# Gate and up projection of a feature tile as seven block products instead of eight, with the order of every engine written out

## The chip, the cores and the metric

The kernel runs on one core of a Trainium2 chip. The time is device microseconds (us) of one execution. Five engines work from queues of their own, each in order: TensorE (PE, its weight loads PEld), VectorE (DVE), ScalarE (ACT), GpSimd (POOL) and SyncE (SP, which only issues transfers here).

## What is computed

Two layers of an encoder on 768 tokens (512 of one batch, 256 of another). Each layer has four mixers, which the change doesn't touch, and then a gated feed-forward block of width 2816 on a model width of 1024:

```python
for l in range(DEPTH):
    ...
    x = x + _rms(mix, p['norm_mix_post'][l])
    h = _rms(x, p['norm_ffn_pre'][l])
    f = (jax.nn.silu(h @ p['ffn_w_gate'][l]) * (h @ p['ffn_w_up'][l])) @ p['ffn_w_down'][l]
    x = x + _rms(f, p['norm_ffn_post'][l])
```

## The kernel before

Each fp32 operand is held as a high part, rounded to the format that PE multiplies (`whi`, `hh`, `ah`), and a low part, the rest (`wlo`, `hl`, `al`). A product is three matmuls: high by high, high by low, low by high. `hh` and `hl` hold the normalised activations, features on the partitions: 8 chunks of 128 by 768 tokens.

The 2816 features are 22 tiles of 128. For each tile `ffn_up` computes gate (`fg`) and up (`fu`), each as 8 chunks by 3 matmuls, for 512 and for 256 tokens: 96 matmuls, 48 of 512 columns and 48 of 256. ACT takes the tanh, DVE makes the product `th`, ACT and DVE split it into `ah` and `al`. Two tiles make a group. `ffn_down` multiplies the group's activations by its down weights, 6 token tiles by 2 halves, 6 matmuls of 512 columns each (`dn`), and DVE adds each result to `y`. So per tile there are 6 such sets of six.

Weights come in pieces of 128x1024 (512 KB), three per tile, into two buffers `raw` by loads on the SP queue. `piece` splits one: ACT copies the high part, then DVE or POOL, in turn, subtracts to get the low part. A `raw` buffer can be loaded again when that subtraction is done.

A scheduler that works by estimates of durations sets the order of every engine. The first group goes through the tokens as 512 and then 256, the last as 256 and then 512, so that the closing norms of the 256 (`post_norm`, `pre_norm`) lie beside the products of the 512. In the middle groups the matmuls of one tile run between the `dn` matmuls of the group before.

Of the kernel before, what the change touches and what calls it, by code (L numbers as in the profile page):

```python
# [82 lines left out]
class Trunk:  # L83
    def __init__(self, ctx, tc, xp, xs, wp, pv, bc, par, cst, scan, strips, yp, ys):
# [1109 lines left out]
    def ffn_up(self, l, f, seqs, wg, wu, th, ah, al):  # L1194
        nc = self.nc
        part = len(seqs) < 2
        pg, pu = {}, {}

        def gate(s):
            t0, n, *_r = SEQS[s]  # L1200
            c = slice(t0, t0 + n)
            nc.scalar.activation(th[:, c], pg[s][:, :n], AF.Tanh, scale=0.5)  # L1202
            nc.vector.scalar_tensor_tensor(out=th[:, c], in0=th[:, c], scalar=1.0, in1=pg[s][:, :n], op0=ALU.add, op1=ALU.mult)

        for s in seqs:
            pg[s] = self.bank("pS" if part else "pb", f"fg{l}_{f}_{s}")
            if not part:
                self.feat_mm(pg[s][:, :SEQS[s][1]], *wg, P, *SEQS[s][:2])
                gate(s)
        for s in seqs:  # L1210
            t0, n, *_r = SEQS[s]
            c = slice(t0, t0 + n)
            pu[s] = self.bank("pS", f"fu{l}_{f}_{s}")
            if part:

                for a in range(0, n, 256):
                    self.feat_mm(pg[s][:, a:a + 256], *wg, P, t0 + a, 256)
                    self.feat_mm(pu[s][:, a:a + 256], *wu, P, t0 + a, 256)
                gate(s)
            else:  # L1220
                self.feat_mm(pu[s][:, :n], *wu, P, t0, n)
            nc.vector.scalar_tensor_tensor(out=th[:, c], in0=th[:, c], scalar=0.5, in1=pu[s][:, :n], op0=ALU.mult, op1=ALU.mult)  # L1222
        c = slice(SEQS[seqs[0]][0], SEQS[seqs[-1]][0] + SEQS[seqs[-1]][1])
# [237 lines left out]
```

## Time and profile before

| | |
|---|---|
| median of the runs | 2311.38 us |
| lowest run | 2308.88 us |
| the profiled execution, its own time | 2307.11 us |
| its span, first to last instruction | 2305.3 us |
| PE busy | 2195.2 us (95%) |
| DVE, ACT, POOL busy | 1278.9, 803.9, 577.7 us |
| mean granted clock of PE | 0.981 |

The span holds, twice, some 580 us of mixers and some 570 us of feed-forward. Busy times of PE are from the start of a matmul to its modelled end; matmuls overlap, so the rate is read from one start to the next. On the other engines a row's duration is the time for which the engine is taken.

### The profile page before, as it was taken

The numbers are of one execution on the slowest core, as the hardware profiler recorded it, in microseconds if no ns is written. First come the engines' busy times: TensorE is split into PE (matmuls) and PEld (weight loads), VectorE is DVE, ScalarE is ACT, GpSimd is POOL, SyncE is SP. The second block draws the span as 40 slices with busy tenths as digits, with TensorE's granted clock in tenths as the row PEclk, the third lists the DMA queues.
The fourth block names the chain that finished last, engine by engine and source line by source line (L and its number), as shares of the span: only waits on it lengthen the run. The fifth ranks groups of instructions, "written<-read, shape, count | busy, mean of one in ns | idle before, by whom it ended". The sixth has DMA issues, their size and how long they took to land.

```text
span 2305.3 us, 44071 instructions
## 1 busy us (share of the span) xinstructions
PE 2195.2 (95%) x18072; PEld 1940.4 (84%) x18072; DVE 1278.9 (55%) x2404; ACT 803.9 (35%) x1675; POOL 577.7 (25%) x521
## 2 busy tenths in 40 slices
PE   7999989999999999999999999898999999999997
PEld 7888888878888888888888888787888888888886
DVE  5597658785623333333566875688764333433345
ACT  4333335665421112221243433455663211221211
POOL 1342213334311111111233422123352111111113
PEclk9999999999999999999999999999999999999999
DMA  4543564345422111222225535634263211122112
...
DMA packets 245096, 240.95 MB, mean 105 GB/s; under 512 B 138784, under 2 KB 191904, under 8 KB 244896
## 3 DMA queue, kind: packets, MB, share of 16 engines
...
q8 instruction: 142, 2.33, 0.4%
...
## 4 chain that ended last, share of the span: by engine, by line
PE 37%; DVE 7%; DMA 3%; issue 1%; POOL 1%; ACT 1%; SPq 0%; DVEq 0%; POOLq 0%; ACTq 0%
PE fg L194 8%; PE fu L194 8%; PE dn L1236 8%; PE dz L194 3%; PE op L183 2%; PE za L183 1%; PE zb L183 1%; DVE nper L460 1%; DVE el L458 1%; PE sd L171 1%; DMA bd<-sl 1%; PE zv L183 1%; PE ob L171 0%; DMA fb<-yd 0%; PE pg L171 0%
## 5 line engine op out<-in xcount | busy, mean ns | idle before, releaser
L165 POOL TENSOR_TENSOR wlo<-raw,whi 128x1024 fp32r<-128x1024 f32 (+1 forms) x108 | 258.5, 2393 | 1049.7 <-ACT whi L162 858.5
L1242 DVE TENSOR_TENSOR y<-y,dn 128x512 f32<-128x512 f32 x240 | 162.7, 686 | 341.7 <-PE dn L1236 341.0
L162 ACT ACTIVATE whi<-raw 128x1024 fp32r<-128x1024 f32 (+1 forms) x222 | 225.3, 1021 | 334.2 <-DMA raw<-in_wp_dram 127.0
L194 PE MATMUL fg<-hl,whi 128*128 128x256 f32 (+1 forms) x768 | 250.3, 326 | 1.4 <-DVE hl L208 1.4
L194 PE MATMUL fg<-hh,whi 128*128 128x256 f32 (+1 forms) x768 | 250.0, 325 | 0.7 <-ACT hh L207 0.7
L194 PE MATMUL fg<-hh,wlo 128*128 128x256 f32 (+1 forms) x768 | 249.0, 325 | 0.0
L194 PE MATMUL fu<-hl,whi 128*128 128x256 f32 (+1 forms) x768 | 248.3, 323 | 0.0
L194 PE MATMUL fu<-hh,whi 128*128 128x256 f32 (+1 forms) x768 | 248.2, 323 | 0.0
L194 PE MATMUL fu<-hh,wlo 128*128 128x256 f32 (+1 forms) x768 | 247.9, 323 | 0.0
L165 DVE TENSOR_TENSOR wlo<-raw,whi 128x1024 fp32r<-128x1024 f32 (+1 forms) x114 | 154.8, 1357 | 132.6 <-ACT whi L162 130.1
L1236 PE MATMUL dn<-whi,ah 128*128 128x512 f32 x528 | 208.9, 396 | 1.9 <-DVE y L1242 1.9
L1236 PE MATMUL dn<-wlo,ah 128*128 128x512 f32 x528 | 209.3, 396 | 0.0
L1236 PE MATMUL dn<-whi,al 128*128 128x512 f32 x528 | 203.8, 393 | 0.0
L194 PEld LDWEIGHTS fg<-hl,whi 128*128 128x128 f32 x768 | 146.1, 190 | 16.0 <-DVE hl L208 1.8
L194 PEld LDWEIGHTS fg<-hh,whi 128*128 128x128 f32 x768 | 146.0, 190 | 15.7 <-ACT hh L207 0.9
L194 PEld LDWEIGHTS fg<-hh,wlo 128*128 128x128 f32 x768 | 146.1, 190 | 13.4
L194 PEld LDWEIGHTS fu<-hh,wlo 128*128 128x128 f32 x768 | 145.4, 189 | 13.7
L194 PEld LDWEIGHTS fu<-hl,whi 128*128 128x128 f32 x768 | 145.6, 190 | 13.6
L194 PEld LDWEIGHTS fu<-hh,whi 128*128 128x128 f32 x768 | 145.6, 190 | 13.1
L1224 ACT ACTIVATE ah<-th 128x768 fp32r<-128x768 f32 (+2 forms) x52 | 38.6, 742 | 298.3 <-DVE th L1222 298.3
L1202 ACT ACTIVATE th<-fg 128x512 f32<-128x512 f32 (+1 forms) x88 | 42.7, 485 | 235.9 <-PE fg L194 235.4
L1236 PEld LDWEIGHTS dn<-whi,al 128*128 128x128 f32 x528 | 98.7, 188 | 23.4
...
## 6 DMA issues: line engine op xcount, KB each, us to landing
...
```

The source lines that it names most:

```text
L162: nc.scalar.activation(hi[:, :n], raw[:, :n], AF.Copy)
L165: eng.tensor_tensor(out=lo[:, :n], in0=raw[:, :n], in1=hi[:, :n].bitcast(F32), op=ALU.subtract)
L171: self.nc.tensor.matmul(ps[c], lhsT=lhsT[:, c], rhs=rhs, start=start, stop=stop)
L183: mm(ps, lhsT=a, rhs=b[:, c:c + ncol], start=i == 0, stop=i == tot - 1)
L194: mm(ps, lhsT=a, rhs=b, start=i == 0, stop=i == 3 * NK - 1)
L458: V.tensor_tensor(out=ev, in0=q[:, j + 1:32, j:j + 1].to_broadcast([96, m, j]), in1=q[:, j:j + 1, 0:j].to_broadcast([96, m, j]), op=ALU.mult)
L460: V.tensor_tensor(out=q[:, j + 1:32, 0:j], in0=q[:, j + 1:32, 0:j], in1=ev, op=ALU.add)
L1202: nc.scalar.activation(th[:, c], pg[s][:, :n], AF.Tanh, scale=0.5)
L1224: nc.scalar.activation(ah[:, c], th[:, c], AF.Copy)
L1236: nc.tensor.matmul(ps, lhsT=a[p], rhs=w[q], start=i == 0, stop=i == tot - 1)
L1242: nc.vector.tensor_tensor(out=yt, in0=yt, in1=ps, op=ALU.add)
```

## The change

Write the gate and up weights of a tile as a block matrix: row blocks gate and up, column blocks chunks 0 to 3 and 4 to 7 of the model width, A11 and A12 for gate, A21 and A22 for up. Write the activations as blocks too: chunks 0 to 3 and 4 to 7 by tokens 0 to 383 and 384 to 767, B11, B12, B21, B22. The four results are then made from seven block products (Winograd's form of Strassen's scheme) in place of eight. Weight sums are S1 = A21 + A22, S2 = S1 - A11, S3 = A11 - A21, S4 = A12 - S2. Activation sums are T1 = B12 - B11, T2 = B22 - T1, T3 = B22 - B12, T4 = T2 - B21. The products are 1: A11 B11, 2: A12 B21, 3: S4 B22, 4: A22 T4, 5: S1 T1, 6: S2 T2, 7: S3 T3. A block product (`block_mm`) is 4 chunks by 3 matmuls of 384 columns.

Tiles 0 and 1 of a layer stay as they were, and tiles 2 to 21 take the new form. In `ffn_sums` the activation sums are formed and split once per layer: POOL and DVE form them and DVE and ACT split them, and T1 is written over B12 in `hh` and `hl` once tiles 0 and 1 have read it. `ffn_units` writes out the order of all engines for tiles 2 to 21. The two raw pieces of a tile, x = (A11, A21) and y = (A22, A12), are split and summed in place: `first` splits A11 (names whr, wlr), `second` splits y (wha, wla), `sums` makes S1 to S4 on POOL in x and y, `third` splits the new x (whb, wlb), `fourth` the new y (whc, wlc). `down_split` splits a half of the down weights (whd, wld), and the two `raw` buffers serve x, y and the down half in turn. The seven products go into six PSUM banks in turn, and DVE and ACT combine them in `fg` and `fu`. The `dn` sets stand one by one between the products. Tiles 2 and 3 have no `dn` sets beside them, as the first group's are done before. The last group's `dn` sets and all closing norms come after tile 21.

```diff
-FFG = 2
+HT = TOK // 2
...
+TS_TAGS = ("Q", "T", "T", "T", "Z", "Z", "V", "D", "D", "Q", "Q")
+XF_ORDER = (0, 1, 2, 4, 5, 3)
...
+    def ffn_sums(self, l):
+        nc = self.nc
+        V, S, A = nc.vector, nc.scalar, nc.gpsimd
+        F = lambda x: x.bitcast(F32)
+        L, R = slice(0, HT), slice(HT, TOK)
+        units = [self.slot(tag, [P, 2, HT], f"ts{l}_{i}", F32R) for i, tag in enumerate(TS_TAGS)]
+        cells = [u[:, j] for u in units for j in range(2)]
+        cells += [self.slot("z", [P, HT], f"tz{l}_{i}", F32R) for i in range(2)]
+        t1s = [self.tmp(f"t1{l}_{j}").rearrange("p (k c) -> p k c", k=2) for j in range(2)]
+        self.tt = {}
+        for k in range(4):
+            t1 = t1s[k // 2][:, k % 2]
+            t2, t3, t4 = [self.slot("R", [P, 512], f"t{n}{l}_{k}")[:, :HT] for n in (2, 3, 4)]
+            for eng, o, r, c in ((A, t1, k, L), (A, t3, k, R), (V, t2, 4 + k, R), (V, t4, 4 + k, L)):
+                eng.tensor_tensor(out=o, in0=F(self.hh[:, r, c]), in1=F(self.hl[:, r, c]), op=ALU.add)
+            A.tensor_tensor(out=t1, in0=t3, in1=t1, op=ALU.subtract)
+            A.tensor_tensor(out=t3, in0=t2, in1=t3, op=ALU.subtract)
+            V.tensor_tensor(out=t2, in0=t2, in1=t1, op=ALU.subtract)
+            V.tensor_tensor(out=t4, in0=t2, in1=t4, op=ALU.subtract)
+            for n, x in ((2, t2), (3, t3), (4, t4)):
+                hi, lo = cells.pop(0), cells.pop(0)
+                S.activation(hi, x, AF.Copy)
+                V.tensor_tensor(out=lo, in0=x, in1=F(hi), op=ALU.subtract)
+                self.tt[n, k] = hi, lo
+        for k in range(4):
+            t1, hi = t1s[k // 2][:, k % 2], self.hh[:, k, R]
+            S.activation(hi, t1, AF.Copy)
+            V.tensor_tensor(out=self.hl[:, k, R], in0=t1, in1=F(hi), op=ALU.subtract)
+    def block_h(self, n, k):
+        if n in (2, 3, 4):
+            return self.tt[n, k]
+        row, c = {1: (k, slice(HT, TOK)), "11": (k, slice(0, HT)), "21": (4 + k, slice(0, HT)), "22": (4 + k, slice(HT, TOK))}[n]
+        return self.hh[:, row, c], self.hl[:, row, c]
...
+    def ff_split(self, eng, tags, name, x):
+        hi, lo = [self.slot(t, [P, x.shape[1]], f"{n}{name}", F32R) for n, t in zip(("wh", "wl"), tags)]
+        self.nc.scalar.activation(hi, x, AF.Copy)
+        eng.tensor_tensor(out=lo, in0=x, in1=hi.bitcast(F32), op=ALU.subtract)
+        return hi, lo
+    def block_mm(self, name, w, j, n):
+        ps = self.bank(("pb", "pb", "pS", "pS", "pT", "pO")[self.nbank % 6], name)[:, :HT]
+        self.nbank += 1
+        i = 0
+        for k in range(4):
+            wh, wl = [x[:, j * 512 + k * P:j * 512 + (k + 1) * P] for x in w]
+            bh, bl = self.block_h(n, k)
+            for a, b in ((wh, bh), (wh, bl), (wl, bh)):
+                self.nc.tensor.matmul(ps, lhsT=a, rhs=b, start=i == 0, stop=i == 11)
+                i += 1
+        return ps
...
+    def down_mm(self, l, g, t, n, act, w):
+        ps = self.bank("pa", f"dn{l}_{g}_{t}_{n}")
+        i = 0
+        for j, (ah, al) in enumerate(act):
+            a = ah[:, t * P:(t + 1) * P], al[:, t * P:(t + 1) * P]
+            b = [x[:, j * 512:(j + 1) * 512] for x in w]
+            for p, q in ((0, 0), (0, 1), (1, 0)):
+                self.nc.tensor.matmul(ps, lhsT=a[p], rhs=b[q], start=i == 0, stop=i == 5)
+                i += 1
+        return ps, g, t, n
...
+    def ffn_units(self, l):
+        nc = self.nc
+        V, S, A = nc.vector, nc.scalar, nc.gpsimd
+        LO, HI = slice(0, 512), slice(512, 1024)
+        L, R = slice(0, HT), slice(HT, TOK)
+        raw, w = {}, {}
+        add = lambda o, x, y, op=ALU.add: V.tensor_tensor(out=o, in0=x, in1=y, op=op)
+        def load(f, i):
+            raw[f, i] = self.ff_raw(l, f // 2, 2 * (f % 2) + i, "raw")
+        def first(f):
+            w[f, "r"] = self.ff_split(V, ("R", "R"), f"r{l}_{f}", raw[f, 0][:, LO])
+        def second(f):
+            w[f, "a"] = self.ff_split(A, ("whi", "wlo"), f"a{l}_{f}", raw[f, 1])
+        def sums(f):
+            x, y = raw[f, 0], raw[f, 1]
+            A.tensor_tensor(out=y[:, LO], in0=x[:, HI], in1=y[:, LO], op=ALU.add)
+            A.tensor_tensor(out=x[:, HI], in0=x[:, LO], in1=x[:, HI], op=ALU.subtract)
+            A.tensor_tensor(out=x[:, LO], in0=y[:, LO], in1=x[:, LO], op=ALU.subtract)
+            A.tensor_tensor(out=y[:, HI], in0=y[:, HI], in1=x[:, LO], op=ALU.subtract)
+        def third(f):
+            w[f, "b"] = self.ff_split(V, ("whi", "wlo"), f"b{l}_{f}", raw.pop((f, 0)))
+        def fourth(f):
+            w[f, "c"] = self.ff_split(V, ("whi", "wlo"), f"c{l}_{f}", raw.pop((f, 1)))
+        def down_load(g, n):
+            raw["d"] = self.ff_raw(l, g, 4 + n, "raw")
+        def down_split(g, n, tags=("X", "X")):
+            w["d", g, n] = self.ff_split(A, tags, f"d{l}_{g}_{n}", raw.pop("d"))
+        load(2, 0)
+        load(2, 1)
+        first(2)
+        second(2)
+        sums(2)
+        third(2)
+        acts, tail, due = {}, None, []
+        def settle(keep=0):
+            while len(due) > keep:
+                self.down_add(*due.pop(0))
+        for f in range(2, NF):
+            nxt = f + 1 if f + 1 < NF else None
+            g, odd = f // 2, f % 2
+            G, U = self.tmp(f"fg{l}_{f}"), self.tmp(f"fu{l}_{f}")
+            c11, c12, c21, c22 = G[:, L], G[:, R], U[:, L], U[:, R]
+            downs = [] if g == 1 else [(t, odd) for t in range(NT)]
+            def mm(n, key, j, h):
+                return self.block_mm(f"p{n}{l}_{f}", w[f, key], j, h)
+            def down(n=1):
+                for _i in range(n):
+                    if downs:
+                        t, half = downs.pop(0)
+                        due.append(self.down_mm(l, g - 1, t, half, acts[g - 1], w["d", g - 1, half]))
+            def tanh(x):
+                th = self.slot("R", [P, 512], f"ft{l}_{f}")[:, :HT]
+                S.activation(th, x, AF.Tanh, scale=0.5)
+                return th
+            def gate(th, x):
+                V.scalar_tensor_tensor(out=x, in0=th, scalar=1.0, in1=x, op0=ALU.add, op1=ALU.mult)
+            def up(x, u):
+                V.scalar_tensor_tensor(out=x, in0=x, scalar=0.5, in1=u, op0=ALU.mult, op1=ALU.mult)
+            wd = (g - 1, 1) if not odd and g > 1 else (g, 0) if odd else None
+            if tail:
+                tail()
+            settle()
+            fourth(f)
+            p = mm(1, "r", 0, "11")
+            S.activation(c12, p, AF.Copy)
+            if nxt:
+                load(nxt, 1)
+            if wd:
+                if "d" not in raw:
+                    down_load(*wd)
+                down_split(*wd)
+            if nxt:
+                load(nxt, 0)
             else:
+                down_load(g, 1)
+            p = mm(2, "a", 1, "21")
+            if odd:
+                down()
+            add(c11, c12, p)
+            th = tanh(c11)
+            p = mm(4, "a", 0, 4)
+            down()
+            settle(1)
+            gate(th, c11)
+            S.activation(c21, p, AF.Copy)
+            p = mm(6, "b", 0, 2)
+            down()
+            settle(1)
+            if nxt:
+                second(nxt)
+            else:
+                down_split(g, 1, ("whi", "wlo"))
+            add(c12, c12, p)
+            p = mm(7, "b", 1, 3)
+            down()
+            settle(1)
+            if nxt:
+                first(nxt)
+                sums(nxt)
+            add(c22, c12, p)
+            add(c21, c22, c21, ALU.subtract)
+            up(c11, c21)
+            p = mm(5, "c", 0, 1)
+            down()
+            settle(1)
+            add(c12, c12, p)
+            add(c22, c22, p)
+            p = mm(3, "c", 1, "22")
+            down(2)
+            if nxt:
+                third(nxt)
+            nwd = (g, 0) if not odd else (g, 1)
+            if nxt:
+                down_load(*nwd)
+            settle(1)
+            add(c12, c12, p)
+            th = tanh(c12)
+            def tail(f=f, g=g, c11=c11, c12=c12, c22=c22, G=G, th=th, gate=gate, up=up):
+                gate(th, c12)
+                up(c12, c22)
+                hi, lo = [self.slot("D", [P, TOK], f"{n}{l}_{f}", F32R) for n in ("ah", "al")]
+                S.activation(hi, G, AF.Copy)
+                V.tensor_tensor(out=lo, in0=G, in1=hi.bitcast(F32), op=ALU.subtract)
+                acts.setdefault(g, []).append((hi, lo))
+        tail()
+        settle()
+        return acts[NF // 2 - 1], [w["d", NF // 2 - 1, n] for n in range(2)]
...
+        self.ffn_sums(l)
+        act = [t[1:] for t in tiles]
+        wd = [self.piece(l, PIECE_FF + 4 + n, tags=("X", "X")) for n in range(2)]
+        for t in range(NT):
+            for n in range(2):
+                self.down_add(*self.down_mm(l, 0, t, n, act, wd[n]))
+        with self.tc.manual_schedule():
+            act, wd = self.ffn_units(l)
+        g_post, g_next = (*self.gains(l, 3), None) if last else self.gains(l, 3, 4)
+        for t in XF_ORDER:
+            for n in range(2):
+                self.down_add(*self.down_mm(l, NF // 2 - 1, t, n, act, wd[n]))
+            x = self.slot(XF_TAG[t], [P, DM], f"xf{l}_{t}")
+            nc.sync.dma_start(out=x, in_=self.x1[t])
...
+    wg, wu = [f[name].reshape(L, NK, P, NF, P).transpose(0, 3, 2, 1, 4) for name in ("ffn_w_gate", "ffn_w_up")]
+    dn = f["ffn_w_down"].reshape(L, NF, P, 2, 512)
+    for i in range(NF):
+        at = PIECE_FF + 6 * (i // 2) + 2 * (i % 2)
+        x, y = wg[:, i], wu[:, i]
+        if i >= 2:
+            x, y = np.concatenate([x[:, :, :4], y[:, :, :4]], axis=2), np.concatenate([y[:, :, 4:], x[:, :, 4:]], axis=2)
+        wp[:, at], wp[:, at + 1] = x.reshape(L, P, -1), y.reshape(L, P, -1)
+    for g in range(NF // 2):
+        for n in range(2):
+            wp[:, PIECE_FF + 6 * g + 4 + n] = np.concatenate([dn[:, 2 * g, :, n], dn[:, 2 * g + 1, :, n]], axis=2)```

DVE in the middle of layer 0. First before, around the end of tile 10; `y` are the sums of the down projection, `wlo` low parts of weights:

```order
L1242 TENSOR_TENSOR y_3_6776<-y_3_6776,dn_8_3_1_9732 128x512
L1222 SCALAR_TENSOR_TENSOR th_10_9772<-th_10_9772,fu_10_1_9870 128x256
L1225 TENSOR_TENSOR al_10_9774<-th_10_9772,ah_10_9773 128x768
L1242 TENSOR_TENSOR y_4_6777<-y_4_6777,dn_8_4_0_9740 128x512
L1242 TENSOR_TENSOR y_4_6777<-y_4_6777,dn_8_4_1_9748 128x512
L1242 TENSOR_TENSOR y_5_6778<-y_5_6778,dn_8_5_0_9756 128x512
L1203 SCALAR_TENSOR_TENSOR th_11_9775<-th_11_9775,fg_11_0_9910 128x512
L1242 TENSOR_TENSOR y_5_6778<-y_5_6778,dn_8_5_1_9764 128x512
L165 TENSOR_TENSOR wlo_70_10021<-raw_70_10018,whi_70_10020 128x1024
```

And DVE after, the second half of tile 11 (`p` are products, `ft` the tanh):

```order
L1245 TENSOR_TENSOR wlr_12_10219<-raw_6_0_10123,whr_12_10218 128x512
L1304 TENSOR_TENSOR fu_11_10091<-fg_11_10090,p_11_10197 128x384
L1304 TENSOR_TENSOR fu_11_10091<-fu_11_10091 128x384
L1371 SCALAR_TENSOR_TENSOR fg_11_10090<-fg_11_10090,fu_11_10091 128x384
L1293 TENSOR_TENSOR y_3_6776<-y_3_6776,dn_4_3_1_10210 128x512
L1304 TENSOR_TENSOR fg_11_10090<-fg_11_10090,p_11_10229 128x384
L1304 TENSOR_TENSOR fu_11_10091<-fu_11_10091,p_11_10229 128x384
L1245 TENSOR_TENSOR wlb_12_10273<-raw_6_0_10123,whb_12_10272 128x1024
L1293 TENSOR_TENSOR y_4_6777<-y_4_6777,dn_4_4_1_10242 128x512
L1304 TENSOR_TENSOR fg_11_10090<-fg_11_10090,p_11_10252 128x384
```

DVE has the low parts of tile 12's weights between the steps of tile 11, and the steps of tile 11 stand behind them.

POOL in the same place. Before, it has only low parts of weights, every second piece:

```order
L165 TENSOR_TENSOR wlo_66_9553<-raw_66_9550,whi_66_9552 128x1024
L165 TENSOR_TENSOR wlo_67_9673<-raw_67_9670,whi_67_9672 128x1024
L165 TENSOR_TENSOR wlo_69_9787<-raw_69_9784,whi_69_9786 128x1024
L165 TENSOR_TENSOR wlo_72_9907<-raw_72_9904,whi_72_9906 128x1024
L165 TENSOR_TENSOR wlo_73_10027<-raw_73_10024,whi_73_10026 128x1024
```

And POOL after, tile 13's pieces, during tile 12 (`raw_6_3` is y, `raw_6_2` is x):

```order
L1245 TENSOR_TENSOR wld_5_1_10312<-raw_5_5_10276,whd_5_1_10311 128x1024
L1245 TENSOR_TENSOR wla_13_10377<-raw_6_3_10309,wha_13_10376 128x1024
L1317 TENSOR_TENSOR raw_6_3_10309<-raw_6_2_10315,raw_6_3_10309 128x512
L1318 TENSOR_TENSOR raw_6_2_10315<-raw_6_2_10315 128x512
L1319 TENSOR_TENSOR raw_6_2_10315<-raw_6_3_10309,raw_6_2_10315 128x512
L1320 TENSOR_TENSOR raw_6_3_10309<-raw_6_3_10309,raw_6_2_10315 128x512
```

Per tile POOL now has two low parts and four sums of 512 columns, all but the first on raw pieces that later steps read.

## Rows read from the trace of the kernel before

**Rows 1.** The page: busy time of each engine; the chain's shares by engine.

```profile
PE 2195.2 (95%) x18072; PEld 1940.4 (84%) x18072; DVE 1278.9 (55%) x2404; ACT 803.9 (35%) x1675; POOL 577.7 (25%) x521
...
PE 37%; DVE 7%; DMA 3%; issue 1%; POOL 1%; ACT 1%; SPq 0%; DVEq 0%; POOLq 0%; ACTq 0%
```

**Rows 2.** Stretches: length, busy PE, PEld, DVE, ACT, POOL, clock, DMA, GB/s.

```profile
580.00:600.00 20.00, 14.66 (x112) 14.05 (x111) 18.87 (x23) 11.20 (x17) 14.31 (x9) 0.91 0.45 146
759.70:810.00 50.30, 50.30 (x265) 43.02 (x265) 17.84 (x25) 9.67 (x13) 7.72 (x3) 1.00 0.21 63
...
1160.00:1180.00 20.00, 14.88 (x91) 13.72 (x90) 16.95 (x30) 10.20 (x19) 6.57 (x8) 0.83 0.18 61
2280.00:2300.00 20.00, 13.06 (x58) 9.50 (x56) 14.82 (x19) 5.23 (x9) 13.13 (x11) 0.95 0.26 92
```

**Rows 3.** PE in order of time, one tile's up projection: start, duration.

```profile
701.71 0.40 PE L194 MATMUL fu<-hh,whi 128*128 128x512 f32 x1
...
702.87 0.39 PE L194 MATMUL fu<-hh,wlo 128*128 128x512 f32 x1
703.10 0.28 PE L194 MATMUL fu<-hh,whi 128*128 128x256 f32 x1
...
704.29 0.28 PE L194 MATMUL fu<-hl,whi 128*128 128x256 f32 x1
```

**Rows 4.** ACT in order of time: the same step of two groups.

```profile
709.40 0.85 ACT L1224 ACTIVATE ah<-th 128x768 fp32r<-128x768 f32 x1 [15.95 <-DVE th L1222]
...
759.70 0.84 ACT L1224 ACTIVATE ah<-th 128x768 fp32r<-128x768 f32 x1 [15.95 <-DVE th L1222]
```

**Rows 5.** Weight pieces in order of time: low parts, loads, high parts, activation's low part.

```profile
720.82 1.22 DVE L165 TENSOR_TENSOR wlo<-raw,whi 128x1024 fp32r<-128x1024 f32 x1
...
721.37 2.93 POOL L165 TENSOR_TENSOR wlo<-raw,whi 128x1024 fp32r<-128x1024 f32 x1 [25.70 <-ACT whi L162]
...
722.07 0.33 SPq L158 DMA_DIRECT2D raw<-in_wp_dram  x1
...
724.33 0.33 SPq L158 DMA_DIRECT2D raw<-in_wp_dram  x1
...
725.71 1.06 ACT L162 ACTIVATE whi<-raw 128x1024 fp32r<-128x1024 f32 x1 [2.35 <-DMA raw<-in_wp_dram]
728.17 1.06 ACT L162 ACTIVATE whi<-raw 128x1024 fp32r<-128x1024 f32 x1 [1.40 <-DMA raw<-in_wp_dram]
...
729.31 2.40 POOL L165 TENSOR_TENSOR wlo<-raw,whi 128x1024 fp32r<-128x1024 f32 x1 [5.00 <-ACT whi L162]
...
733.87 0.95 DVE L1225 TENSOR_TENSOR al<-th,ah 128x768 fp32r<-128x768 f32 x1
```

**Rows 6.** DVE and POOL in the same two stretches.

```profile
585.40 3.83 POOL L230 TENSOR_TENSOR y<-y,gain 128x512 f32<-128x512 f32 x2
...
588.69 0.67 DVE L1177 TENSOR_TENSOR y<-y,ob 128x512 f32<-128x512 f32 x1
...
1125.52 2.57 POOL L230 TENSOR_TENSOR yg<-y,gain 128x512 f32<-128x512 f32 x2 [4.37 <-DVE y L1242]
...
1126.83 2.33 DVE L165 TENSOR_TENSOR wlo<-raw,whi 128x1024 fp32r<-128x1024 f32 x1 [0.20 <-ACT whi L162]
```

**Rows 7.** Steps of 512 and 256 columns; in two rows duration is minimum/median/maximum in ns.

```profile
718.70 0.60 ACT L1202 ACTIVATE th<-fg 128x512 f32<-128x512 f32 x1 [8.45 <-PE fg L194]
...
722.98 0.39 ACT L1202 ACTIVATE th<-fg 128x256 f32<-128x256 f32 x1 [1.68 <-PE fg L194]
...
728.45 0.69 DVE L1222 SCALAR_TENSOR_TENSOR th<-th,fu 128x512 f32<-128x512 f32 x1 [0.42 <-PE fu L194]
731.31 0.42 DVE L1222 SCALAR_TENSOR_TENSOR th<-th,fu 128x256 f32<-128x256 f32 x1 [2.18 <-PE fu L194]
...
L1242 DVE TENSOR_TENSOR y<-y,dn x240: 670/686/690, 689.1 to 2296.9; 128x512 f32<-128x512 f32 x120
...
L230 POOL TENSOR_TENSOR yg<-y,gain x40: 1276/1297/1800, 542.9 to 2297.7; 128x512 f32<-128x512 f32 x40
```

More of the change, by code (lines that the diff above doesn't have):

```diff
@@ L1191, in mixers @@
                     (START, 1.0, self.out(l)), (START, DENSE_RATE, self.op(l))])
-    def ffn_up(self, l, f, seqs, wg, wu, th, ah, al):
+    def ffn_sums(self, l):
         nc = self.nc
[L1196 to L1223, printed above, removed]
@@ new lines, in ffn_up @@
+    def ffn_up(self, l, f, s, wg, wu, th, ah, al):
+        nc = self.nc
+        t0, n, *_r = SEQS[s]
+        c = slice(t0, t0 + n)
+        pg, pu = self.bank("pS", f"fg{l}_{f}_{s}"), self.bank("pS", f"fu{l}_{f}_{s}")
+        for a in range(0, n, 256):
+            self.feat_mm(pg[:, a:a + 256], *wg, P, t0 + a, 256)
+            self.feat_mm(pu[:, a:a + 256], *wu, P, t0 + a, 256)
+        nc.scalar.activation(th[:, c], pg[:, :n], AF.Tanh, scale=0.5)
+        nc.vector.scalar_tensor_tensor(out=th[:, c], in0=th[:, c], scalar=1.0, in1=pg[:, :n], op0=ALU.add, op1=ALU.mult)
+        nc.vector.scalar_tensor_tensor(out=th[:, c], in0=th[:, c], scalar=0.5, in1=pu[:, :n], op0=ALU.mult, op1=ALU.mult)
@@ new lines, in ffn @@
+        tiles = [(self.tmp(f"th{l}_{f}"), self.slot("D", [P, TOK], f"ah{l}_{f}", F32R), self.slot("D", [P, TOK], f"al{l}_{f}", F32R)) for f in range(2)]
+        ws = []
+        for f in range(2):
+            ws.append([self.piece(l, PIECE_FF + 2 * f + i, tags=("Q", "Q") if f and i else ("whi", "wlo")) for i in range(2)])
+            self.ffn_up(l, f, 0, *ws[f], *tiles[f])
+        for f in range(2):
+            self.ffn_up(l, f, 1, *ws[f], *tiles[f])
+        self.ffn_sums(l)
+        act = [t[1:] for t in tiles]
@@ new lines, in ffn @@
+        wd = [self.piece(l, PIECE_FF + 4 + n, tags=("X", "X")) for n in range(2)]
[5 more added lines that the diff above has]
+        g_post, g_next = (*self.gains(l, 3), None) if last else self.gains(l, 3, 4)
+        late = None
+        for t in XF_ORDER:
[3 more added lines that the diff above has]
+            nc.sync.dma_start(out=x, in_=self.x1[t])
+            if last:
+                dst = self.yp[0, t * P:(t + 1) * P, :] if t < 4 else self.ys[0, (t - 4) * P:(t - 3) * P, :]
+            else:
+                dst = self.xd[t]
+            self.post_norm(self.y[t], x, t, g_post, True, dst)
+            if not last:
@@ L1284, in ffn @@
                 if late:
                     self.pre_norm(*late, g_next)
+                late = x, t
+        if late:
+            self.pre_norm(*late, g_next)
     def run(self):
```

66 lines of the change are left out of this document (12 added, 54 removed).

## The prediction

> **What bounds the kernel now.** I read the page first: PE is busy 95% of the span and has the largest share of the chain that ended last, and DVE, with 55%, is the next [rows 1]. An average can hide stages, so I read the stretches next. In the middle of the feed-forward block, over the 50.30 us between the same step of two groups [rows 4], PE is busy 50.30 of 50.30 us at clock 1.00, DVE 17.84, ACT 9.67, POOL 7.72 [rows 2]. So a group of two tiles is bound by PE alone, 25.15 us per tile, and all else hides. At the block's start and at its end this is not so: PE is busy 14.66 of 20 us at 580, 14.88 of 20 at 1160, 13.06 in the last 20, and DVE is then the busiest beside it [rows 2]. What the change takes from PE is worth its full time in the middle as long as the other engines still fit under PE.
>
> **What it saves on PE.** From start to start, five steps of 512 columns take 702.87 - 701.71 = 1.16 us, 0.232 each, and ten of 256 columns take 1.19 us, 0.119 each [rows 3]. The two give a line, and 384 columns on it take 0.176. A tile's gate and up cost 48 x (0.232 + 0.119) = 16.85 us before and 7 x 12 x 0.176 = 14.78 after, so 2.07 less. With the 36 down matmuls (36 x 0.232 = 8.35) a tile takes 25.2 before, which agrees with the 25.15 of rows 4, and 23.13 after. For 20 tiles in 2 layers the saving is **83 us**, 3.6%, and no more than that.
>
> The Trainium skill has another spacing, TensorE: Matmul & The Clock Gate, section Back-to-back issue gap: columns / 2.4 + 2.5 ns on a warm array, so 0.216, 0.109 and 0.163 us for 512, 256 and 384. By it the saving would be 1.95 us a tile or 78 in all. The trace disagrees (0.232 at clock 1.00), and I use the trace.
>
> **What it adds on the other engines, in the middle.** Steps of 384 columns lie between those of 512 and 256 [rows 7]: 0.555 on DVE, 0.49 on ACT. Per tile DVE has 6 additions to y (0.686 each), 7 combinations and 4 gate steps of 384 (11 x 0.555), low parts of 512 (0.69) and of 1024 twice (1.22) and the activation's low part (0.95): 14.3 us. POOL has two low parts (2.40) and four sums of 512 (1.28, the fastest of its two-input steps of that size): 9.9 us. ACT has about 7.6. Each fits under 23.1.
>
> They also get in each other's way. A DVE low part that takes 1.22 alone [rows 5] took 2.33 when it began at 1126.83 under two POOL steps that ran to 1128.09, that is, it ended 1.07 after them; an addition with one operand in PSUM took 0.67 in the middle of POOL's steps at 585.40, which were themselves stretched to 3.83 from 2.57 by DVE steps with two SBUF inputs [rows 6]. So I let POOL's steps and DVE's steps with two SBUF inputs exclude each other, step by step. Together they are 9.9 + 6.8 = 16.7 us per tile, still under 23.1.
>
> What can bound is a **loop from tile to tile** that doesn't pass PE. The down half's low part frees its `raw` buffer for the next tile's x. x must land, be split, be summed, be split again. On DVE, in order, the current tile's last combinations stand behind that split, and behind those the next tile's fourth split, which with its POOL neighbour frees the buffers again. The terms, from rows 5 and 7: POOL low part 2.40; load 3.65 (issue at 722.07 to the first use at 725.71; the next one took 3.84); ACT 0.60; DVE low part of 512 0.69; three POOL sums 3.84 with two DVE steps let in between 1.11; ACT 1.06; DVE low part 1.22 with 0.2 until the fourth sum ends; additions to y, one or two, 1.03; combination 0.555; tanh 0.49; two gate steps 1.11; ACT 0.84; low part 0.95; addition 0.69; fourth split 1.22; some 20 hand-offs of 0.03 as 722.04 to 722.07, 0.6. The sum is **22.3 us against PE's 23.1**. PE still bounds, by 0.8. Half of the hand-offs may take twice as long and loads do vary by 0.2, so I put 0.2 us per tile for 34 tiles, 7 us, and keep 0 and what rival A says as ends.
>
> **What it adds at the start of a layer's new tiles.** Tiles 2 and 3 have no down matmuls: PE has 14.8 us each, but the loop still takes 20.5 from tile 3 to 4 (the sum without the additions to y) and about 19.5 from 2 to 3 (no down piece there, so the y piece's 2.40 on POOL stands before the sums instead). From tile 2's fourth split to tile 5's that is 19.5 + 20.5 + 22.3 = 62.3, where PE has 14.8 + 14.8 + 23.1 = 52.7: 9.6 lost. Tile 2's own fourth split comes 10.9 us into its products (high part 1.06, low part 2.40, four sums 5.1, 1.06, 1.22), in a later tile 5.3 us into them (tanh to fourth split above): another 5.6. I take 15 per layer, **30 us**. If DVE and POOL overlapped freely in the sums, a round would be 2.6 shorter; the ends are 7 and 20 per layer.
>
> **Activation sums.** Per chunk DVE has 8 steps of two SBUF inputs (0.555) and POOL 4 of about 1.0 (three quarters of 1.28), 8.4 us that exclude each other, 34 per layer. They can begin when the last token is normalised, by then some 15 of the first group's 50 us of PE work is done, so 36 are left to cover them. In the same time come the group's own low parts (two of 0.69, two of 0.42) and tile 2's first pieces, 8 us. 34 + 8 - 36 leaves **6 per layer, 12 us**; the ends are 0 and 15 per layer. ACT's copies of the down results wait among its copies for the sums, which is in the 6.
>
> **Ends of the layers.** Before, two of the six token tiles close beside the last products of the others; now all six close after them. In layer 0 a token tile costs DVE eight steps of 512 (0.69) and about 1 us of waiting for POOL, 6.5, with 2.8 of down matmuls as cover: 2 x 3.7 = 7.4. In the last layer there are four such steps, 3.3 against 2.8, 1 us. Together **8 us**, between 0 and 15. PE's clock was 0.83 in such a stretch [rows 2], which costs little where DVE is late.
>
> **Sum.** -83 + 7 + 30 + 12 + 8 = -26 on the profiled execution's 2307.1 (span 2305.3 and 1.8 around it): 2281. The median of the runs is 4.3 above that execution, so I forecast **2285 us**.
>
> **Rivals.**
> A. The loop becomes the bound and the kernel is slower. Place: fourth split to fourth split in tiles 5 to 20. Price: 34 us for each us beyond 23.1; without the 7 the sum is -33, so the kernel is slower than before from a loop of 24.1, and by over 2% (46 us) from 25.4. For it: the sum has 20 links, and 4% on all of them already passes PE; the load of y is issued right behind, so that two are under way; every additional DVE step under a POOL step adds to it. Against: each link is read from this trace and was 22.3. At 25.5: -33 + 34 x 2.4 = +49, 2360 us.
> B. The covers hold better and the kernel is faster by over 2%. The exclusion is weaker in short steps, so that rounds shorten by 2.6, the activation sums vanish under the first group, the closing norms cost nothing: -83 + 14 = -69, 2242. Half way there is 2263. For it: the middle's engines are far from full. Against: rows 6 show the exclusion at full length for steps of 512 too.
> C. 384 columns don't lie on the line and cost PE as much as 512. Then a tile's products take 84 x 0.232 = 19.5, 2.6 more than before, and the kernel 2311 + 104 + 50 = 2465. Against it: 256 columns cost 0.51 of 512.
>
> **Chances.** The measurement can't well tell less than about 2% from no change, that is, between 2265 and 2357. The forecast and its neighbourhood (-46 to +46) 0.64, B 0.24, A 0.10, C 0.02. Faster 0.24, same 0.64, slower 0.12. The range: the low end is B's 2242 with 8 us of the bounds given back, 2250; the high end a loop of 24.7 us (-33 + 54 and 4.3 for the median, 2333) with the upper bound of the activation sums half used, 2342.
>
> **What would show it.** In the profile after, products of 384 columns should start 0.176 apart; in the middle of a layer the first product of a tile should follow that of the tile before in 23.1 to 23.4 us with PE busy throughout, from tile 5 on; between tiles 2 and 5 about 68 us where PE has 52.7; PE idle in front of `dn` around the activation sums, put down to ACT's copies of `y`, some 6 us; a closing stretch in which DVE is full and PE waits. If the tile period is 24 or more and the fourth split or `al` is what `dn` waits for, A is right. If tiles 2 to 5 take under 60, my exclusion was too strict. What would make me wrong beyond these: a load that waits on the SP queue behind another that isn't ready, since SP is in order too and y's load stands behind the down half's.

## The result and the profile after

The changed kernel takes 2283.99 us (median of 4 runs, 2280.82 to 2284.89) against 2311.38 of before in the same comparison: ratio 0.9879, 95% interval 0.986 to 0.9899, so 27.4 us or 1.2% faster. Two executions that took far longer than the rest (5318.89 us of before, 2536.69 of a later kernel) are left out of all medians. The forecast was 2285. The profiled execution took 2280.8 (span 2279.0).

The page of after, busy time and the chain's shares (against [rows 1]):

```profile
PE 2132.7 (94%) x17400; PEld 1937.1 (85%) x17400; DVE 1608.7 (71%) x2804; ACT 920.4 (40%) x1863; POOL 905.1 (40%) x733
...
PE 64%; DVE 18%; DMA 7%; issue 4%; POOL 3%; ACT 3%; SPq 1%; DVEq 0%; POOLq 0%; ACTq 0%
```

PE lost 62.5 us of busy time, DVE gained 330 and POOL 327. The chain of before could be followed back through half of the span only (its shares add up to 50%), so its 7% for DVE are some 14% of what was followed, against 18% of after. That is a hint that PE is less often what ends last; where, the stretches of after tell (columns as in [rows 2]; the second is two tiles in the middle):

```profile
580.00:600.00 20.00, 16.96 (x123) 16.79 (x122) 19.63 (x23) 10.38 (x17) 12.40 (x8) 0.83 0.48 170
764.26:810.55 46.29, 46.29 (x241) 43.05 (x240) 32.26 (x42) 14.83 (x20) 22.27 (x12) 1.00 0.22 69
688.54:692.40 3.86, 3.64 (x11) 3.31 (x12) 3.79 (x5) 0.00 (x0) 3.62 (x4) 0.57 0.00 0
1120.00:1140.00 20.00, 15.32 (x69) 11.24 (x67) 17.34 (x27) 11.06 (x19) 17.55 (x16) 1.00 0.45 144
2260.00:2280.00 20.00, 4.96 (x19) 3.23 (x18) 11.69 (x17) 3.45 (x6) 10.41 (x10) 0.82 0.54 184
```

Two tiles take 46.29 us with PE busy for all of it, at clock 1.00: 23.15 per tile against 25.15 [rows 2, 4]. DVE has 16.1 per tile there and POOL 11.1, so both still fit. At 1120, in the closing norms of layer 0, they do not: DVE is busy 17.34 of 20 us, POOL 17.55, and PE waits.

PE of after in order of time: waits for copies of y, the first product of tiles 2 to 7, and one product of 384 columns from first step to last:

```profile
644.56 0.50 PE L1284 MATMUL dn<-whi,ah 128*128 128x512 f32 x1 [1.77 <-ACT y L1291]
...
651.32 0.50 PE L1284 MATMUL dn<-whi,ah 128*128 128x512 f32 x1 [0.89 <-ACT y L1291]
...
652.81 0.34 PE L1257 MATMUL p<-hh,whr 128*128 128x384 f32 x1
...
670.32 0.33 PE L1257 MATMUL p<-hh,whr 128*128 128x384 f32 x1
...
688.54 0.45 PE L1257 MATMUL p<-hh,whr 128*128 128x384 f32 x1 [2.56 <-ACT whr L1244]
...
717.96 0.34 PE L1257 MATMUL p<-hh,whr 128*128 128x384 f32 x1
...
741.12 0.34 PE L1257 MATMUL p<-hh,whr 128*128 128x384 f32 x1
...
764.26 0.34 PE L1257 MATMUL p<-hh,whr 128*128 128x384 f32 x1
...
780.40 0.34 PE L1257 MATMUL p<-hh,whc 128*128 128x384 f32 x1
...
782.34 0.34 PE L1257 MATMUL p<-hh,wlc 128*128 128x384 f32 x1
```

Eleven steps take 1.94 us, 0.176 each, as the line through [rows 3] said. From tile 5 on the tiles follow in 23.16 and 23.14. From tile 2 to tile 5 it is 65.15 us, where PE has 52.7. What PE waits for around there, added up (us in total, times, longest):

```profile
PE dn L1284 <- ACT y L1291: 2.7, 2, 1.8
PE p L1257 <- ACT whr L1244: 2.6, 1, 2.6
PE dn L1284 <- DVE y L1293: 1.7, 1, 1.7
PE dn L1284 <- ACT ah L1445: 1.5, 1, 1.5
PE p L1257 <- ACT whb L1244: 1.1, 1, 1.1
...
```

The first row is the activation sums, the others are the rounds of the loop. (A round is the time from one tile's fourth split to the next tile's.) The stretches of the feed-forward block can be set against each other between marks that all kernels have. From the first `fg` to the last `dz` (products of layer 1's mixers), before took 671.3 and, in a second trace of it (last experiment), 667.7; after 654.8. From the last `ob` of layer 1 to the end, before 577.0 and 578.0, after 558.6. Against the mean of the two traces of before the blocks are 14.7 and 18.9 shorter, 33.6 together.

### The profile page after: what moved, and what is told of

Same layout as the page of the kernel before. It is cut to its first block, busy times and chain, and to the rows that moved or that the text cites. A ratio compares the mean times of both kernels' runs of the same rounds, so it can differ in the third digit from the quotient of the medians.

```text
span 2279.0 us, 43655 instructions
## 1 busy us (share of the span) xinstructions
PE 2132.7 (94%) x17400; PEld 1937.1 (85%) x17400; DVE 1608.7 (71%) x2804; ACT 920.4 (40%) x1863; POOL 905.1 (40%) x733
## 4 chain that ended last, share of the span: by engine, by line
PE 64%; DVE 18%; DMA 7%; issue 4%; POOL 3%; ACT 3%; SPq 1%; DVEq 0%; POOLq 0%; ACTq 0%
PE p L1257 22%; PE dn L1284 13%; PE dz L197 5%; PE op L186 4%; DMA raw<-in_wp_dram 3%; PE za L186 2%; DVE el L461 2%; PE zb L186 2%; DVE nper L463 2%; DVE wlo L168 1%; PE sd L174 1%; PE ob L174 1%; PE fg L197 1%; PE fu L197 1%; PE ptb L767 1%
## 5 line engine op out<-in xcount | busy, mean ns | idle before, releaser
L1245 POOL TENSOR_TENSOR wld<-raw,whd 128x1024 fp32r<-128x1024 f32 x40 | 104.1, 2603 | 345.6 <-ACT whd L1244 345.6
L1293 DVE TENSOR_TENSOR y<-y,dn 128x512 f32<-128x512 f32 x240 | 163.2, 681 | 95.2 <-PE dn L1284 95.0
L1284 PE MATMUL dn<-whd,ah 128*128 128x512 f32 x480 | 192.3, 401 | 18.1 <-DVE y L1293 9.7
L1284 PE MATMUL dn<-whd,al 128*128 128x512 f32 x480 | 191.7, 399 | 1.0 <-DVE al L1446 1.0
L1284 PE MATMUL dn<-wld,ah 128*128 128x512 f32 x480 | 190.3, 396 | 0.0
L168 POOL TENSOR_TENSOR wlo<-raw,whi 128x1024 fp32r<-128x1024 f32 (+1 forms) x48 | 108.6, 2263 | 172.3 <-ACT whi L165 145.5
L1257 PE MATMUL p<-ts,whb 128*128 128x384 f32 x640 | 165.4, 339 | 2.1 <-ACT whb L1244 2.1
L1245 POOL TENSOR_TENSOR wla<-raw,wha 128x1024 fp32r<-128x1024 f32 x40 | 96.0, 2400 | 107.4 <-ACT wha L1244 107.4
L165 ACT ACTIVATE whi<-raw 128x1024 fp32r<-128x1024 f32 (+1 forms) x102 | 99.7, 978 | 90.3 <-DMA raw<-in_wp_dram 34.4
L1304 DVE TENSOR_TENSOR fg<-fg,p 128x384 f32<-128x384 f32 x160 | 87.7, 548 | 60.7 <-PE p L1257 60.3
L1244 ACT ACTIVATE whb<-raw 128x1024 fp32r<-128x1024 f32 x40 | 42.5, 1062 | 208.4 <-POOL raw L1319 208.4
L1257 PEld LDWEIGHTS p<-ts,whb 128*128 128x128 f32 x640 | 116.8, 188 | 9.0 <-ACT whb L1244 2.8
L1284 PEld LDWEIGHTS dn<-whd,ah 128*128 128x128 f32 x480 | 90.8, 189 | 36.3 <-DVE y L1293 15.7
L186 PE MATMUL zc<-whi,hh 128*128 128x256 f32 x384 | 113.8, 298 | 1.5 <-ACT zc L785 0.9
L186 PE MATMUL zc<-whi,hl 128*128 128x256 f32 x384 | 111.6, 292 | 0.0
L1284 PEld LDWEIGHTS dn<-whd,al 128*128 128x128 f32 x480 | 90.8, 189 | 24.3 <-DVE al L1446 2.8
L186 PE MATMUL zc<-wlo,hh 128*128 128x256 f32 x384 | 111.4, 292 | 0.0
L1257 PE MATMUL p<-ts,wlb 128*128 128x384 f32 x320 | 108.0, 337 | 1.5 <-DVE wlb L1245 1.5
L1257 PE MATMUL p<-hh,wlc 128*128 128x384 f32 x320 | 107.6, 336 | 1.2 <-DVE wlc L1245 1.2
L1257 PE MATMUL p<-hh,whc 128*128 128x384 f32 x320 | 107.8, 337 | 0.0
```

The costliest lines, as they stand in the source:

```text
L165: nc.scalar.activation(hi[:, :n], raw[:, :n], AF.Copy)
L168: eng.tensor_tensor(out=lo[:, :n], in0=raw[:, :n], in1=hi[:, :n].bitcast(F32), op=ALU.subtract)
L186: mm(ps, lhsT=a, rhs=b[:, c:c + ncol], start=i == 0, stop=i == tot - 1)
L1245: eng.tensor_tensor(out=lo, in0=x, in1=hi.bitcast(F32), op=ALU.subtract)
L1257: self.nc.tensor.matmul(ps, lhsT=a, rhs=b, start=i == 0, stop=i == 11)
L1284: self.nc.tensor.matmul(ps, lhsT=a[p], rhs=b[q], start=i == 0, stop=i == 5)
```

## Experiments

All medians stand against 2283.99 of after, unless said otherwise. Before, measured anew beside each group of runs, took 2311.0 to 2313.6, and the runs of one kernel spread over some 4 us, so a difference of 3 us or less can't be told from none.

**The loop, made longer.** POOL repeats the down half's low part once (`range(1)`), or twice:

```diff
-            w["d", g, n] = self.ff_split(A, tags, f"d{l}_{g}_{n}", raw.pop("d"))
+            x = raw.pop("d")
+            hi, lo = w["d", g, n] = self.ff_split(A, tags, f"d{l}_{g}_{n}", x)
+            for _i in range(1):
+                A.tensor_tensor(out=lo, in0=x, in1=hi.bitcast(F32), op=ALU.subtract)
```

> The low part of each down half is computed twice on POOL (same values), which holds its raw buffer 2.40 us longer and so lengthens the loop from tile to tile by 2.40. Prediction's loop of 22.3 us: it becomes 24.7 against PE's 23.1, so PE falls behind by 1.55 in each of 16 rounds after tile 5 of a layer, less some 4.5 us by which al and the low parts run ahead of PE, and the rounds from tile 3 to 5 cost 4.8 more: about +25 us per layer, +50, 2334 us. Theory from the trace after (fourth split to fourth split 18.4, 19.6, 21.1 from tile 2 to 5, each 1.1 under the prediction): the loop is 21.1, so 23.5 here, 0.35 over PE, nearly all of it inside the 4.5: +4.8 to +6 per layer, about +12, 2296. No loop at all (POOL is only 40% busy): 0, 2284.

> The same low part is computed three times on POOL, so the loop is 4.80 us longer. Loop of 22.3: 27.1, 16 x 3.95 less 4.5 and 9.6 in the first rounds, +68 per layer, +137, 2421 us. Loop of 21.1: 25.9, 16 x 2.75 less 4.5 and 9.6, +49 per layer, +98, 2382; tile period 25.9. No loop: 0, 2284. POOL's busy time is then 14.7 of 26 us per tile, so its rate bounds nothing.

Measured: 2295.08 (+11) and 2396.77 (+113). With one repeat PE is still busy throughout the middle, with two it isn't. Windows of the middle, one kernel each (columns as above):

```profile
800.00:1080.00 280.00, 280.00 (x1453) 259.75 (x1452) 199.45 (x253) 90.11 (x121) 164.00 (x85) 1.00 0.21 68
```

```profile
782.00:1088.00 306.00, 287.75 (x1432) 261.94 (x1431) 195.96 (x249) 86.04 (x117) 190.08 (x96) 0.96 0.19 61
```

In the second kernel, `al` of two tiles six apart (DVE in order of time):

```profile
936.97 0.96 DVE L1449 TENSOR_TENSOR al<-fg,ah 128x768 fp32r<-128x768 f32 x1 [0.91 <-ACT ah L1448]
...
1090.86 0.96 DVE L1449 TENSOR_TENSOR al<-fg,ah 128x768 fp32r<-128x768 f32 x1 [0.91 <-ACT ah L1448]
```

One down half's low part with its two repeats, in the same kernel (POOL in order of time; L1335 is the repeats):

```profile
861.87 2.64 POOL L1245 TENSOR_TENSOR wld<-raw,whd 128x1024 fp32r<-128x1024 f32 x1 [7.65 <-ACT whd L1244]
864.59 5.08 POOL L1335 TENSOR_TENSOR wld<-raw,whd 128x1024 fp32r<-128x1024 f32 x2
```

The `al` rows give 25.65 per tile. The repeats put the end of the low part off by 5.16, not by the 4.80 that I had added up. Less that, the loop is some 20.5 us, not 22.3, and under PE by 2.6. POOL is busy 62% there, so it is the loop and not POOL's rate that bounds. The theory's loop of 21.1 (its last round is 21.5 in the trace) gave 2296 and 2382: the first came true, in the second the period was 0.25 shorter, yet the time 15 longer; that the low parts' lead of 4.5 us would be used up first was not seen.

**Six `dn` sets kept for tiles 2 and 3**, three in each, so that PE has work there:

```diff
-            downs = [] if g == 1 else [(t, odd) for t in range(NT)]
+            downs = [(t, 1) for t in range(3 * odd, 3 * odd + 3)] if g == 1 else [(t, odd) for t in range(NT)]
...
```

> Six of the first group's twelve dn sets (second half of the down weights) run in tiles 2 and 3, three in each, instead of ahead of tile 2. If tiles 2 to 5 are slow because PE has too little work there, the 8.35 us fill idle time: -8 per layer, about -17, 2267 us. If they are slow because the rounds of the loop start only when the activation sums are done (whr of tile 2 at 651.6 stands on ACT behind the last copy of the sums), PE only idles earlier: 0 to -3 in all, 2281 to 2284, with PE idle for some 8 us ahead of tile 2.

Measured: 2280.67 (-3). PE's waits there (as above) begin with one long one:

```profile
PE p L1257 <- ACT whr L1244: 9.4, 1, 9.4
PE dn L1284 <- DVE y L1293: 1.9, 1, 1.9
...
```

The idle time only moved ahead of tile 2: the rounds start when the activation sums let them, and PE's work does not fill them.

**Tile 2's first split ahead of the activation sums**, in two versions; the second moves the line that loads and splits the first group's down pieces (`wd = ...`) ahead of these two:

```diff
+        raw = {(2, i): self.ff_raw(l, 1, i, "raw") for i in range(2)}
+        w = {(2, "a"): self.ff_split(nc.gpsimd, ("whi", "wlo"), f"a{l}_2", raw[2, 1])}
         self.ffn_sums(l)
...
```

> The loads of tile 2's raw pieces and the split of its y piece (wha, wla) stand ahead of the activation sums in the program, not behind; POOL has 12 us idle between its first sums and the next (619 to 631). If the rounds start when tile 2's splits are done, they start earlier by the 2.4 of wla and by the sums that POOL can begin beside DVE's last steps, 4 to 5 us per layer: -8 to -10, 2275 us. If POOL and DVE together are at their rate in that stretch, so that the step only displaces the sums, 0, 2284.

> As the run before with tile 2's pieces loaded and its y piece split ahead of the activation sums, but the first group's down pieces are loaded ahead of them, so that these don't wait for a raw buffer. Theory that the rounds of tiles 2 to 5 run in a chain from the end of the activation sums: the fourth split of tile 2 comes 4.7 us earlier (657.5, as in the run before, against 662.2), and tile 5's first product with it: -4.7 per layer, -9, 2275 us. If POOL and DVE are at their rate there: 0, 2284.

Measured: 2317.02 (+33) and 2285.24 (+1). The first version shows an unwanted effect: x and y of tile 2 hold both `raw` buffers, the down pieces are loaded only at 657.5, and PE waits 21.1 us for `whr` with the `dn` sets queued behind. In the second that is gone, but `wlc` of tile 2 comes 71.6 us after the first `fg` against 74.4, and in layer 1 71.1 after the last `ob` against 72.1; tile 5's products gain 1.4 and 0.2. My expectation fell: in layer 0 the last step of the sums ends 67.1 us after the first `fg` against 64.5 of after, so the early step pushed the sums back.

**No activation sums**: `ffn_sums` is replaced by a table of blocks of `hh` and `hl`.

```diff
-        for k in range(4):
-            t1 = t1s[k // 2][:, k % 2]
...
+        self.tt = {(n, k): (self.hh[:, k + 4 * (n < 4), c], self.hl[:, k + 4 * (n < 4), c])
+                   for k in range(4) for n, c in ((2, slice(HT, TOK)), (3, slice(HT, TOK)), (4, slice(0, HT)))}
```

> Leaves out the activation sums T1 to T4 and their splits (the products read blocks of hh and hl in their place), and nothing else. The prediction took the sums (12 us in all) and the start of tiles 2 to 5 (30) as two costs: then only the idle time ahead of the first group's dn goes, 3.0 per layer by the trace, 2278 us. If the sums also set when the rounds of tiles 2 to 5 begin, most of the 12.5 us per layer lost there goes too: -12 to -15 per layer, 2256 us.

Measured: 2257.07 (-27). PE then waits 3.6 us in the same stretch of layer 0 (waits as above, all of them):

```profile
PE dn L1258 <- DVE y L1267: 1.7, 1, 1.7
PE dn L1258 <- ACT ah L1419: 1.6, 1, 1.6
PE dn L1258 <- DVE al L1420: 0.3, 1, 0.3
```

Tile 2's pieces are split under the first group, `wlc` of tile 2 comes 25 to 27 us earlier, and what the rounds lose is mostly covered by `dn` sets that are still to do. The two blocks of the traces are 24 shorter. So the sums cost 12 to 13 per layer, not the 3 that PE waits for them directly.

**The sums in an order by hand**, among the last gate steps of tiles 0 and 1 (`ffn_up` and `ffn_sums` cut into pieces):

```diff
+        with self.tc.manual_schedule():
+            g10 = self.ffn_up(l, 1, 0, *ws[1], *tiles[1])
+            chunk(0)
+            g10()
+            g01 = self.ffn_up(l, 0, 1, *ws[0], *tiles[0])
+            chunk(1)
+            g01()
...
```

> All work as in the changed kernel; only the order of the activation sums and of the last gate steps of tiles 0 and 1 is written out: chunk 0's sums stand ahead of tile 1's gate on DVE, ACT and POOL, chunk 1's and 2's between the later gates. In the trace after, DVE is idle for 11.0 us between 615.0 and 628.5, waiting for those gates with the sums queued behind. If the sums are a chain that these waits push out, they end up to 8 us earlier, PE no longer waits for the copies of y (3.0), and tiles 2 to 5 start earlier: -5 to -8 per layer, 2268 to 2274 us. If the early split's result holds here too (what moves forward only displaces other steps): 0, 2284.

Measured: 2273.36 (-11), ratio to before 0.983 (0.9812 to 0.9848). `wlc` of tile 2 in layer 0, of after (first `fg` at 587.8) and of this kernel (first `fg` at 589.3):

```profile
662.19 1.23 DVE L1245 TENSOR_TENSOR wlc<-raw,whc 128x1024 fp32r<-128x1024 f32 x1
```

```profile
657.22 1.23 DVE L1247 TENSOR_TENSOR wlc<-raw,whc 128x1024 fp32r<-128x1024 f32 x1
```

It comes 6.5 us earlier in layer 0 and 5.8 in layer 1, tile 5's first product 5.9 and 5.7: the gain of 10.6 is there. Unlike the early split the order by hand adds no step ahead of the sums; it puts their steps into DVE's waits for the gates, and their last one ends 58.2 us after the first `fg`, not 64.5.

**The ends.** The last tile's activation in two halves, three of the last `dn` sets earlier, other buffers for two loads:

```diff
-XM_TAG, XF_TAG = "ZXZXZX", "VZZVZZ"
+XM_TAG, XF_TAG = "ZXZXZX", "VZZVXX"
...
             up(c11, c21)
+            if not nxt:
+                act = [self.slot("D", [P, TOK], f"{n}{l}_{f}", F32R) for n in ("ah", "al")]
+                S.activation(act[0][:, L], c11, AF.Copy)
+                V.tensor_tensor(out=act[1][:, L], in0=c11, in1=act[0][:, L].bitcast(F32), op=ALU.subtract)
+                acts[g].append(act)
...
```

> Only the last tile of a layer changes: its activation is split in two halves of tokens, the first half as soon as up(c11, c21) is done, and three of the last group's dn sets (tokens 0 to 255) stand between products 5 and 3 and behind 3; the loads of x for the closing norms of token tiles 4 and 5 take X buffers, not Z. If the closing stretch is a chain that begins when al of tile 21 is done (2243.8) and then takes 4.2 us per token tile, it begins some 4 us earlier and loses the 3.2 us for which DVE waited for a load at 2270: -6 to -7 in the last layer and -4 in the first, 2273 us. If DVE and POOL are at their rate from tile 21 on: -3 for the load alone, 2281.

> The early split, the changed ends, and six of the first group's dn sets kept for tiles 2 and 3, together. By the chain the first two are worth -9 and -10. With the chain begun 4.7 us earlier the kept dn sets no longer only move idle time: PE reaches tile 2 that much earlier, another 2 to 4 per layer: -25, 2259 us. If they only add, -22, 2262; if none of them holds, 2280.

> The hand order of the sums and the changed ends of the layers together. The ends were worth 2 us in the median (4.3 in the last layer's stretch). If the two add: 2266 to 2272 us, ratio to before 0.980 to 0.983.

Measured: 2282.47 (-2), 2278.23 (-6), and 2272.06 for the last, ratio to before 0.9818 (0.9802 to 0.9834), the fastest of the kernels that leave nothing out; its difference to the hand order alone is inside the intervals. It lies at the upper edge of what was expected; the second, put at 2259 to 2262, falls short with its early split. For the changed ends I had said -10: from `wlc` of tile 21 to the end the last layer takes 51.9 us in all three against 56.2 of after (54.2 to 56.2 in the kernels with the old end), and the wait for a load (3.2) is gone. In layer 0 nothing can be read: to the last `dz` it is 152.4, 149.0 and 149.6, and kernels with the old end have 150.1 to 158.5.

**No gain in the closing norms:**

```diff
-            g = self.slot("D", [P, 512], f"yg{t}_{i}") if apart else y[:, c]
-            nc.gpsimd.tensor_tensor(out=g, in0=y[:, c], in1=gain[:, c], op=ALU.mult)
+            g = self.slot("D", [P, 512], f"yg{t}_{i}") if apart and not closing else y[:, c]
+            if not closing:
+                nc.gpsimd.tensor_tensor(out=g, in0=y[:, c], in1=gain[:, c], op=ALU.mult)
...
```

> Leaves out the multiplication by the gain in the closing norms of the feed-forward block (two POOL steps of 512 per token tile, yg), and nothing else. In the trace after, DVE's closing steps xf and xn take 0.74 us alone and 1.0 to 1.8 where a yg step runs on POOL, 4.4 us more than alone in the last layer and 4.6 in the first. If the closing stretch is long because POOL and DVE hold each other up: -4 and -4.5, with all xf steps at 0.75, 2275 us. If it is a chain of PE, norm (ACT, POOL) and loads and the longer steps lie in its waits: 0 to -2, 2282.

Measured: 2272.55 (-11). The closing steps of after, in the last layer (DVE in order of time):

```profile
2258.11 2.96 DVE L234 SCALAR_TENSOR_TENSOR xf<-yg,q1r,xf 128x512 f32<-128x512 f32 x2
...
2262.20 3.17 DVE L234 SCALAR_TENSOR_TENSOR xf<-yg,q2r,xf 128x512 f32<-128x512 f32 x2
...
2273.16 1.41 DVE L234 SCALAR_TENSOR_TENSOR xf<-yg,q5r,xf 128x512 f32<-128x512 f32 x2 [3.19 <-DMA xf<-x]
2274.49 1.41 DVE L234 SCALAR_TENSOR_TENSOR xf<-yg,q3r,xf 128x512 f32<-128x512 f32 x2
```

And the same steps without the gain (durations minimum, median, maximum in ns):

```profile
L235 DVE SCALAR_TENSOR_TENSOR xf<-y,q1r,xf x4: 742/744/747, 1122.6 to 2253.3; 128x512 f32<-128x512 f32 x4
L235 DVE SCALAR_TENSOR_TENSOR xf<-y,q2r,xf x4: 746/747/751, 1127.1 to 2256.3; 128x512 f32<-128x512 f32 x4
```

A pair takes 2.96 and 3.17 us where POOL's `yg` runs and 1.41 where it doesn't; without `yg` all are at 0.75. From `wlc` of tile 21 both ends are 6 us shorter (50.3 against 56.2, 144.1 against 150.1), where I had said 4 to 4.5; in the last layer it is 4 to 6, as kernels with the old end have 54.2 to 56.2.

That is the price of the gain's steps, and not what the change added. Before has the same stretched pairs in its last layer:

```profile
2289.82 2.80 DVE L231 SCALAR_TENSOR_TENSOR xf<-yg,q0r,xf 128x512 f32<-128x512 f32 x2
...
2293.80 3.14 DVE L231 SCALAR_TENSOR_TENSOR xf<-yg,q1r,xf 128x512 f32<-128x512 f32 x2
...
2297.66 2.43 DVE L231 SCALAR_TENSOR_TENSOR xf<-yg,q2r,xf 128x512 f32<-128x512 f32 x2
```

All twelve `xf` steps of that layer add up to 13.1 us in before, 13.4 in after and 9.0 without the gain; the 24 `xf` and `xn` steps of layer 0 to 20.5, 23.2 and 18.0. So some 3 us of the stretch are new. No run leaves the gain out of before.

**Before, once more:**

> The kernel before once more, for a second trace of it. Between the first dz to end the layer and the last ob the layer 1 mixers took 471.8 us before and 477.8 after, and in eight variants of after 473.4 to 482.3. If the 6 us are the new order of the same instructions, this trace shows 472 again, with the clock at 0.98 to 1.00 from the last sd on; if they are chance of one execution, anything between 472 and 480.

Measured: 2311.99, layer 1's mixers 477.2 us and the first `fg` at 587.3, as in after (477.8, 587.8). Where the two traces of before differ, the last 85.1 us up to the last `ob` (columns as above; each starts in its own trace):

```profile
1643.20:1728.30 85.10, 79.53 (x708) 75.87 (x707) 54.23 (x107) 50.92 (x124) 41.80 (x37) 1.00 0.51 162
```

```profile
1647.10:1732.20 85.10, 79.39 (x668) 75.59 (x667) 51.56 (x98) 47.74 (x112) 38.88 (x34) 0.94 0.49 157
```

In 85.1 us the second executes 668 matmul records, the first 708, at granted clocks of 0.94 and 1.00. So before itself takes either time, and a cost of the change in the mixers is not shown; one trace of each kernel is too few to rule out a few us.

## Why the prediction was right, term by term

- **PE, -83.** 0.176 per step and 23.15 per tile: right. By the measured periods (25.15 less 23.15, 40 tiles) it is 80, as the tile of before was 25.15 and not the 25.2 of the sum.
- **The loop, +7.** Below 1: 23.145 against 23.13. The sum of 22.3 was about 1.8 too long. The other engines of after where the loop passes from one tile to the next:

```profile
834.97 0.85 ACT L1445 ACTIVATE ah<-fg 128x768 fp32r<-128x768 f32 x1 [1.28 <-DVE fg L1371]
...
837.04 1.05 ACT L1244 ACTIVATE whd<-raw 128x1024 fp32r<-128x1024 f32 x1
...
837.32 1.22 DVE L1245 TENSOR_TENSOR wlc<-raw,whc 128x1024 fp32r<-128x1024 f32 x1
...
838.16 2.64 POOL L1245 TENSOR_TENSOR wld<-raw,whd 128x1024 fp32r<-128x1024 f32 x1 [9.23 <-ACT whd L1244]
```

  POOL's `wld` starts behind ACT's `whd`, beside `wlc` and not behind it: 2.34 after `ah` ends, where I had 2.86 for `al`, the addition and the fourth split. The load took 3.42 (840.83 to 844.25) for 3.65, the three sums 4.6 for 4.95. These make 1.1; the rest isn't settled.
- **Start of the new tiles, +30.** 65.15 and 65.2 where PE has 52.7: 12.5 per layer, +25. From fourth split to fourth split the rounds took 18.4, 19.6 and 21.5 for 19.5, 20.5 and 22.3.
- **Activation sums, +12.** 3.0 per layer in front of `dn` from start to start, +6. But the prediction took this and the start as two costs, and they are one: the sums end when they end, and the rounds start there. Without the sums 27 of the 31 went (24 by the blocks of the traces), and moving the sums alone by some 6 us moved tile 5 by as much.
- **Layer ends, +8.** Mis-sized, by 7 or more. The two blocks got 33.6 shorter where PE saved 80, so 46.4 came back; less 0.5, 25 and 6 that leaves 15 for the ends (18 if PE saved the forecast's 83), uncertain by some 4, as the two traces of before differ. For the last layer I took 3.3 of DVE per token tile against 2.8 of cover. Two things were longer. DVE waited 3.2 in the last layer and 1.1 in layer 0 for a load of `x`, which no closing step of before does; with other buffers for two of the loads the wait is gone. And the `xf` and `xn` steps that now close behind the products are stretched under POOL, as the exclusion of [rows 6] would have said had I applied it there: some 3 us more than in before. These make 7, about what the term was short of; that each lengthened the end by its full size is argued and not shown.

The terms measured, -80 + 1 + 25 + 6 + 15 = -33, lie 7 under the forecast's -26: start, sums and loop cost less, the ends more. (The ends are what the others leave, so the sum is no check on them.) In the two traces that I set against each other the blocks are 34.9 shorter, the mixers 8.6 longer and the whole is 26.3 shorter, which is the forecast to the decimal. The medians say 27.4. So the mechanism was right in PE, in the loop that stays under PE and in the place of the costs; that the time came out 1 us from the forecast is luck, as terms that were 3 to 7 off, and the mixers' chance, cancelled.

Rival A did not come about, but its place was real: with 5.2 us more the loop bounds, and 113 less some 18 in the first rounds is 95 for 2.5 us beyond 23.1, 38 per us where I had 34. (Some 12 of the 95 lie outside the rounds: 4 in the mixers and 8 behind tile 21 of layer 0, for which no run shows a cause. Without them it is 33.) PE then waits not for `al` but for `dn` banks, in the window from 782 to 1088 that was shown above:

```profile
PE dn L1284 <- DVE y L1293: 18.2, 6, 3.2
```

The additions to `y` stand on DVE behind the next tile's splits. Rival B needed the covers to hold; of all runs only the one without sums (2257.07) lies in its 2242 to 2263. Rival C fell with 0.176.
